# Decay masks from matrix products, or from differences of running sums: one change to a two-layer recurrent trunk

## The chip, the core and the metric

The kernel runs as one program on one core of a Trainium2 chip. A core has a matrix engine (TensorE, "PE" in the profile, with its weight loads shown apart as "PEld"), a vector engine (VectorE, "DVE"), an activation engine (ScalarE, "ACT"), a general engine (GpSimd, "POOL") and a sequencer that here only issues transfers (SyncE, "SP"). Each engine works through its own list of instructions in order and waits on semaphores for the others. The metric is the device time of one execution in microseconds (us); lower is better. Before the change it is 2958.59 us, the median of three runs (2957.11 to 2960.16).

## The reference

Two decoder layers are computed for 256 tokens of width 2048, in float32. Layer 0 mixes an HGRN2 head group with a gated-DeltaNet head group (8 heads), layer 1 is a Mamba-2 SSD mixer (64 heads in 8 groups of 8). Each layer then cross-attends into 256 memory tokens and applies a SwiGLU feed-forward block.

Both the DeltaNet and the SSD part need, for each head, a decay mask: with log-decays `g` of the tokens, token `i` sees token `j <= i` with the factor `exp(g[j+1] + ... + g[i])`, and tokens after it not at all. The reference writes that as a difference of running sums, chunk by chunk:

```python
acum = jnp.cumsum(ac, axis=-1)
lower = jnp.tril(jnp.ones((CHUNK, CHUNK), bool))
lmat = jnp.exp(jnp.where(lower, acum[..., :, None] - acum[..., None, :], -jnp.inf))
cb = jnp.einsum('zbign,zbjgn->zbgij', cc, bc)
y_diag = jnp.einsum('zbgrij,zbjgrp->zbigrp', cb[:, :, :, None] * lmat, xc)
```

The kernel covers the 256 tokens as two halves of 128 (index `a`), so it needs three 128x128 blocks per head: half 0 on half 0, half 0 on half 1, and half 1 on half 1. A block has the earlier token `j` on the partitions and the later token `i` along the row.

## The kernel before

Most of the program is a stream of weight tiles. `wtiles` (L160 and on) loads 512 KB of raw weights through SP's queue into `wr`, ACT rounds them to the reduced float32 format (`wh`, the cast recorded at L157), and DVE takes the remainder (`wl`, the subtraction recorded at L125). There are four buffers of each. `xstat` multiplies 128 tokens of activations, also split into two parts (`u`), with every tile: per tile of 1024 columns a row, twelve matmuls of 128x512 into two accumulators `acc` (three products, two token halves, two k). So a weight tile can be rounded at most four tiles ahead of the matmuls that use it. All matmuls of the helper `mm` have line L122, transposes of activations L285.

Work between the weight matmuls goes to PSUM tiles `mx` (three buffers). The order on each engine is not written out by hand. The scheduler of the framework simulates a timeline while the program is recorded and emits each engine's list in that order; instructions with no stated order can move past each other, and a changed operation can thus move others.

The decay masks are made by two functions. `decay_parts(gT, n)` runs once in each mixer (n = 8 heads in DeltaNet, 64 in SSD), after the log-decays `gT` (128 tokens x 2 halves x n) are known. It splits `gT` into `gh` and `gl`, makes one column per head `cj` (the sum of the decays after token j in half 0), and for half 1 a row of running sums per head, which goes through DRAM (`rows`). `decays(gs, h0, pool_e)` makes the masks `E` (128 x 4 heads x 3 blocks x 128) of four heads. It is called twice in DeltaNet (tile `D`) and sixteen times in SSD: twice per group of 8 heads, into `D` and then into `MD`. The middle block is a broadcast of the running sums, loaded by POOL's queue straight into `E`, plus the column as the bias of an exponential (four of 128x128, L421). The two others are matrix products: DVE multiplies the decays by a triangular matrix `le`, once for `gh` and once for `gl` (four products of 128x512 into `tmp`, L125), and PE multiplies a strictly triangular matrix `gt_r` into them (four matmuls of 128x512, `mx<-tmp,mr`), so that the sums of the stretches come out in PSUM; ACT exponentiates them into `E` (L416, L419). `gt_r` and a matrix of ones lie in the tile `mr`.

In SSD, `group(g, bct)` then multiplies `E` by the products `cb` (one 128x1536 product on DVE per four heads, written `D<-D,b` or `MD<-MD,b`), and PE multiplies it with the group's values (`mx<-D,w` and `mx<-MD,w`). DVE adds the result to the skip term (`X<-cv,cols,mx`), multiplies by the gate, and ACT and DVE split it into a new `u` for the output projection, which runs after groups 3 and 7. The tag `tmp` has two buffers, and in SSD only `decays` uses it. Each group takes 16 weight tiles, 8 for the values and 8 for the gate.

Of the kernel before, what the change touches and what calls it, by code (L numbers as in the profile page):

```python
# [9 lines left out]
F32 = mybir.dt.float32  # L10
F32R = mybir.dt.float32r
U32 = mybir.dt.uint32
I32 = mybir.dt.int32
AF = mybir.ActivationFunctionType
ALU = mybir.AluOpType
# [20 lines left out]


C_ID, C_GT, C_LE = 0, 128, 256
C_LV = 384
LEVELS = (1, 2, 4, 8, 16, 32, 64)  # L40


# [26 lines left out]
def constants():  # L69
    a = np.arange(P)[:, None]  # L70
    b = np.arange(P)[None, :]
    parts = [a == b, a > b, a <= b]
    for s in LEVELS:
        parts.append(((b // s) % 2 == 1) & (a // s == b // s - 1))
    return np.concatenate([p.astype(np.float32) for p in parts], axis=1)
# [3 lines left out]
def trunk(ctx: ExitStack, tc: tile.TileContext, A: dict, out: bass.AP):  # L79
# [20 lines left out]
    le = cst[:, C_LE:C_LE + P]  # L100
    eps = cp.tile([P, 1], F32, name="eps")
    pool.memset(eps, EPS)
    mr = cp.tile([P, 2, P], F32R, name="mr")
    gt_r, ones_r = mr[:, 0, :], mr[:, 1, :]
    gt, ones = gt_r.bitcast(F32), ones_r.bitcast(F32)

    def later(ins):

        return tc.keep_in_program_order(ins)

    def constants_in():
        later(nc.sync.dma_start(cst, A["cst"][:, 0:C_LV]))
        later(nc.sync.dma_start(cols[:, KT:], A["cols"][:, KT:]))
        dve.tensor_copy(gt_r, cst[:, C_GT:C_GT + P])
        dve.tensor_scalar(ones_r, ident, 0.0, 1.0, op0=ALU.mult, op1=ALU.add)

    def col(name, i=0, n=1):
        o = COLS[name][0] + i
# [2 lines left out]
    def mm(o, lhsT, rhs, start=True, stop=True):  # L121
        return pe.matmul(o, lhsT=lhsT, rhs=rhs, start=start, stop=stop, skip_group_check=True)  # L122

    def tt(e, o, a, b, op):
        e.tensor_tensor(o, a, b, op=op)  # L125
# [4 lines left out]
    def t4(tag, shape, dt=F32):  # L130
        return mp.tile(shape, dt, name=tag, tag=tag, bufs=BUFS.get(tag, 1))

    def psb(shape=None):
        return pm.tile(shape or [P, 512], F32, name="mx", tag="mx")
# [21 lines left out]
    def split(hi, lo, src):  # L156
        act.copy(hi, src)  # L157
        tt(dve, lo, src, hi.bitcast(F32), ALU.subtract)
# [57 lines left out]
    class SquareSum:  # L216
# [17 lines left out]
        def column(self, n):  # L234

            r = cp.tile([P, 2], F32, name="r", tag="r", bufs=2)
            ps = psb([P, 2])
            for a in range(2):
                mm(ps[:, a:a + 1], self.s[:, a * P:(a + 1) * P], ones[:, 0:1])
            rsqrt(r, ps, n)  # L240
            return r

# [157 lines left out]

    def decays(gs, h0, pool_e):

        gs, cj, gr = gs
        E = t4(pool_e, [P, 4, 3, P])
        nc.gpsimd.dma_start(E[:, :, 1, :], gr[h0:h0 + 4, :].partition_broadcast(P))
        gle = []
        for a in range(2):
            g2 = t4("tmp", [P, 2, 4, P], F32R)
            for q in range(2):
                tt(dve, g2[:, q], gs[q][:, a, h0:h0 + 4].bitcast(F32).unsqueeze(2).to_broadcast([P, 4, P]),  # L410
                   le.unsqueeze(1).to_broadcast([P, 4, P]), ALU.mult)
            gle.append(g2)
        p00, p11 = psb([P, 4, P]), psb([P, 4, P])
        mm(p00, gt_r, gle[0][:, 0], True, False)
        mm(p00, gt_r, gle[0][:, 1], False, True)
        act.activation(E[:, :, 0, :], p00, AF.Exp)  # L416
        mm(p11, gt_r, gle[1][:, 0], True, False)
        mm(p11, gt_r, gle[1][:, 1], False, True)
        act.activation(E[:, :, 2, :], p11, AF.Exp)  # L419
        for m in range(4):  # L420
            act.activation(E[:, m, 1, :], E[:, m, 1, :], AF.Exp, bias=cj[:, h0 + m:h0 + m + 1])  # L421
        return E

    def decay_parts(gT, n):


        gh, gl = t4("gh", [P, 2, n], F32R), t4("gl", [P, 2, n], F32R)
        split(gh, gl, gT)
        cj = t4("cj", [P, n])
        ps = psb([P, n])  # L430
        mm(ps, gt, gT[:, 0, :])
        dve.tensor_copy(cj, ps)
        gr, gd = t4("gr", [n, P]), dp.tile([n, P], F32, name=f"rows{n}")
        ps = psb([n, P])
        mm(ps, gT[:, 1, :], le)
        act.copy(gr, ps)
        nc.gpsimd.dma_start(gd, gr)
        return (gh, gl), cj, gd

    def head_norm(o_ps, gate, yT, eps):  # L440

# [36 lines left out]
    def hybrid(N, nxt):  # L478
# [47 lines left out]
        def gdn(g):  # L526
# [3 lines left out]
            for j, dst in ((1, 0), (0, 1)):  # L530
                c = kq[:, :, dst, :]
                conv_in(j, g, c)
                if j and not heads:
                    heads.extend(small_heads())
                elif not j:
                    E = decays(heads[0], 4 * g, "D")
                    for b in (0, 2):
                        tt(dve, E[:, :, b, :], E[:, :, b, :], le.unsqueeze(1).to_broadcast([P, 4, P]), ALU.mult)
                act.activation(c, c, AF.Silu)
                sq = t4("tmp", [P, 4, T])  # L540
                act.activation(sq, c, AF.Square)
                for a in range(2):
                    for m in range(4):
                        mm(nps[:, dst, a, m:m + 1], sq[:, m, a * P:(a + 1) * P], ones[:, 0:1])
            if g == 0:
                levels_in()

# [500 lines left out]
```

## Time and profile before

| what | value |
| --- | --- |
| median of three runs | 2958.59 us (2957.11 to 2960.16) |
| the profiled execution, time | 2957.01 us |
| the profiled execution, span | 2955.2 us |
| mean granted TensorE clock | 0.998 |
| PE busy | 2929.2 us (99% of the span) |
| PE weight loads busy | 2432.1 us (82%) |
| DVE busy | 1781.8 us (60%) |
| ACT busy | 1518.5 us (51%) |
| transfers, mean | 182 GB/s |

The span runs from the first to the last instruction; the profiled time holds another 1.8 us around it. A matmul's recorded duration is longer than its share of the engine, since matmuls overlap: in a stretch of back-to-back work, what one costs is read from the distance between starts, not from the duration in the groups. The mask work lies in two places: at about 56 to 75 us and around 257 us (DeltaNet, groups 0 and 1), and from about 1440 to 2030 us (SSD).

### The profile page before, as it was taken

Reading aid. Unit: us, or ns where it says so; the run is one execution under the profiler, and the core shown is the slowest. Engines: PE = TensorE matmul, PEld = TensorE weight load, DVE = VectorE, ACT = ScalarE, POOL = GpSimd, SP = SyncE. Lnnn points to the kernel's source line nnn. Section 1 sums busy time; section 2 is a strip of 40 time slices with the busy share of each in tenths; the row PEclk is TensorE's granted clock in tenths of the full one; section 3 lists DMA queues with packets and bytes.
Section 4 is the critical chain, followed back from the end, with each engine's and each line's share of the span. In section 5 each row is a group of like instructions: output and inputs, shape, how many; then the busy total and the mean of one; then the engine's idle time right before and its main releaser. Section 6 shows DMA issues by size and latency. Waiting matters only on the chain.

```text
span 2955.2 us, 36490 instructions
## 1 busy us (share of the span) xinstructions
PE 2929.2 (99%) x13916; PEld 2432.1 (82%) x13916; DVE 1781.8 (60%) x2320; ACT 1518.5 (51%) x1942; POOL 34.3 (1%) x57
## 2 busy tenths in 40 slices
PE   9999999999999999999999999999999999999998
PEld 7888888788888888888888788878888888888887
DVE  6676768766554445545677746777665454455455
ACT  7445446555443443444667645766554444443444
POOL 0000000000000000000000000000000000000000
PEclk9999999999999999999999999999999999999999
DMA  8555544456665566665655566555666666666664
GB/s 284 169 173 158 183 137 134 143 181 190 189 189 193 192 188 191 194 190 184 187 171 165 171 193 185 170 164 168 195 193 185 192 188 193 191 190 192 193 187 148
DMA packets 153664, 538.11 MB, mean 182 GB/s; under 512 B 16920, under 2 KB 23200, under 8 KB 153488
## 3 DMA queue, kind: packets, MB, share of 16 engines
q1 hardware_dynamic: 150096, 526.15, 57.0%
q0 software_dynamic: 2976, 9.35, 1.0%
q8 instruction: 109, 1.79, 0.2%
q14 instruction: 67, 0.55, 0.1%
q10 hardware_dynamic: 416, 0.27, 0.0%
HBM read 531.21 MB, written 4.49 MB: 181 GB/s over the span
## 4 chain that ended last, share of the span: by engine, by line
PE 97%; DVE 1%; ACT 1%; DMA 1%; issue 0%; SPq 0%; DVEq 0%; ACTq 0%; POOLq 0%
PE acc L122 89%; PE mx L122 5%; PE mx L285 1%; PE tn L285 1%; DMA wr<-in_hy_w_in 0%; DVE wl L125 0%; ACT wh L157 0%; PE mx L884 0%; DVE tmp L125 0%; DMA D<-rows 0%; ACT b L313 0%; DMA rows<-gr 0%; DVE b L128 0%; PE mx L453 0%; DVE h L125 0%
## 5 line engine op out<-in xcount | busy, mean ns | idle before, releaser
L122 PE MATMUL acc<-wh,u 128*128 128x512 f32 (+1 forms) x7904 | 2448.5, 389 | 6.9 <-ACT wh L157 6.5
L125 DVE TENSOR_TENSOR wl<-wr,wh 128x1024 fp32r<-128x1024 f32 x980 | 1197.9, 1224 | 990.3 <-ACT wh L157 986.6
L122 PEld LDWEIGHTS acc<-wh,u 128*128 128x128 f32 x7904 | 1474.4, 188 | 306.3 <-ACT wh L157 6.5
L157 ACT CAST wh<-wr 128x1024 fp32r<-128x1024 f32 x980 | 1029.1, 1052 | 1140.1 <-PE acc L122 1089.9
L122 PE MATMUL acc<-wl,u 128*128 128x512 f32 (+1 forms) x3952 | 1538.6, 389 | 0.9 <-DVE wl L125 0.8
L122 PEld LDWEIGHTS acc<-wl,u 128*128 128x128 f32 x3952 | 743.4, 188 | 150.5 <-DVE wl L125 2.0
L128 DVE SCALAR_TENSOR_TENSOR cv<-tn,cols,cv 128x255 f32<-128x255 f32 (+2 forms) x120 | 57.5, 479 | 10.9 <-ACT cv L363 8.0
L125 DVE TENSOR_TENSOR h<-h,acc 128x512 f32<-128x512 f32 (+1 forms) x92 | 57.7, 657 | 9.8 <-PE acc L122 9.5
L371 ACT ACTIVATE raw<-acc,r 128x512 f32<-128x512 f32 x66 | 43.5, 685 | 29.9 <-PE acc L122 28.2
L128 DVE SCALAR_TENSOR_TENSOR u<-mx,cols,u 128x256 fp32r<-128x256 f32 x96 | 43.1, 478 | 6.6 <-ACT u L306 5.4
L285 PE MATMUL tn<-cst,raw 128*128 128x128 f32 x272 | 45.3, 272 | 0.4 <-DVE vt L128 0.4
L306 ACT ACTIVATE u<-mx,cols 128x256 fp32r<-128x256 f32 x80 | 35.0, 469 | 20.9 <-PE mx L285 17.8
L285 PEld LDWEIGHTS tn<-cst,raw 128*128 128x128 f32 x272 | 34.4, 140 | 9.9 <-issue 0.8
L125 DVE TENSOR_TENSOR u<-mx,u 128x512 fp32r<-128x512 f32 x48 | 31.0, 684 | 13.3 <-ACT u L157 13.3
L157 ACT CAST u<-mx 128x512 fp32r<-128x512 f32 x48 | 26.0, 593 | 17.2 <-PE mx L285 10.6
L313 ACT ACTIVATE b<-h 128x512 f32<-128x512 f32 x48 | 29.9, 624 | 1.3 <-DVE h L128 1.3
L125 DVE TENSOR_TENSOR tmp<-gh,cst 128x512 fp32r<-128x512 f32 x36 | 24.6, 686 | 7.6 <-PE mx L122 7.6
L122 PEld LDWEIGHTS mx<-tmp 128*128 128x128 f32 x240 | 28.1, 192 | 0.6
L122 PE MATMUL mx<-tmp 128*128 128x64 f32 (+1 forms) x240 | 27.9, 273 | 0.0
L285 PE MATMUL mx<-cst,h 128*128 128x128 f32 x160 | 25.6, 272 | 0.0
L128 DVE SCALAR_TENSOR_TENSOR X<-cv,cols,mx 128x256 f32<-128x256 f32 x32 | 14.0, 478 | 18.5 <-PE mx L122 18.5
L122 PE MATMUL mx<-tmp,mr 128*128 128x512 f32 x72 | 24.9, 427 | 0.0
(272 smaller groups left out, 1254.5 us busy)
## 6 DMA issues: line engine op xcount, KB each, us to landing
wr<-in_ffn_w_gate SPq DMA_DIRECT2D x176, 512.0 KB, 3.7
wr<-in_ffn_w_up SPq DMA_DIRECT2D x176, 512.0 KB, 3.7
wr<-in_ffn_w_down SPq DMA_DIRECT2D x176, 512.0 KB, 3.6
wr<-in_ssd_w_in SPq DMA_DIRECT2D x162, 512.0 KB, 3.7
wr<-in_hy_w_in SPq DMA_DIRECT2D x130, 512.0 KB, 3.8
wr<-in_ssd_w_out SPq DMA_DIRECT2D x64, 512.0 KB, 3.7
wr<-in_hy_w_out SPq DMA_DIRECT2D x32, 512.0 KB, 3.7
wr<-in_xa_wq SPq DMA_DIRECT2D x16, 512.0 KB, 3.7
```

What stands on the lines that cost most here:

```text
L122: return pe.matmul(o, lhsT=lhsT, rhs=rhs, start=start, stop=stop, skip_group_check=True)
L125: e.tensor_tensor(o, a, b, op=op)
L128: dve.scalar_tensor_tensor(o, a, s, b, op0=op0, op1=op1)
L157: act.copy(hi, src)
L285: pe.transpose(ps[:, x, a * P:(a + 1) * P], src[a][:, c * P:(c + 1) * P], ident)
L306: act.activation(hi[:, c], ps[:, x], AF.Copy, scale=g)
L313: act.activation(t4("b2", [P, 512]), src[:, a], AF.Square, accum_out=self.ss[:, a, nb:nb + 1])
L371: act.activation(o[a], accs[a], func, scale=r[:, a:a + 1])
```

## The change

Both functions are rewritten. `decay_parts` now makes running sums that restart every 64 tokens: as rows for both halves (`gr`, n x 2 x 128, through DRAM as before), and as six columns per head (`gs`): for each half and each chunk of 64 later tokens, minus the running sum of token j where j lies in that chunk, the sum left after j in its own chunk where j lies in the chunk before, and for half 0 on half 1 the sum of all that lies between j and the chunk. Four constant matrices produce them on PE in plain float32: `csum`, `rest` and `half` are new constants, `gt` existed. They lie in the tile `cst`, and a new transfer on POOL's queue brings the three. `mr` and the two DVE instructions that filled it are gone; `ones` is a column set by POOL.

`decays` loads the rows of both halves into a `tmp` tile `R` (512 KB on chip in place of 256 KB), adds the columns with two DVE instructions (1024 and 512 elements a row), clamps the first and third block at zero with a third (1024 elements), and takes one exponential over 1536 elements. What lies above the diagonal is clamped and later masked as before. No matmul is left in it.

```diff
 def constants():
     a = np.arange(P)[:, None]
     b = np.arange(P)[None, :]
-    parts = [a == b, a > b, a <= b]
+    same = a // 64 == b // 64
+    parts = [a == b, a > b, a <= b, (a <= b) & same, (a > b) & same, (a < 64) & (b >= 0)]
...
-    mr = cp.tile([P, 2, P], F32R, name="mr")
-    gt_r, ones_r = mr[:, 0, :], mr[:, 1, :]
-    gt, ones = gt_r.bitcast(F32), ones_r.bitcast(F32)
+    gt, csum, rest, half = (cst[:, c:c + P] for c in (C_GT, C_SUM, C_REST, C_HALF))
+    ones = cp.tile([P, 1], F32, name="ones")
+    pool.memset(ones, 1.0)
...
     def constants_in():
-        later(nc.sync.dma_start(cst, A["cst"][:, 0:C_LV]))
+        later(nc.sync.dma_start(cst[:, 0:C_SUM], A["cst"][:, 0:C_SUM]))
+        nc.gpsimd.dma_start(cst[:, C_SUM:], A["cst"][:, C_SUM:C_LV])
         later(nc.sync.dma_start(cols[:, KT:], A["cols"][:, KT:]))
-        dve.tensor_copy(gt_r, cst[:, C_GT:C_GT + P])
-        dve.tensor_scalar(ones_r, ident, 0.0, 1.0, op0=ALU.mult, op1=ALU.add)
...
     def decays(gs, h0, pool_e):
-        gs, cj, gr = gs
-        E = t4(pool_e, [P, 4, 3, P])
-        nc.gpsimd.dma_start(E[:, :, 1, :], gr[h0:h0 + 4, :].partition_broadcast(P))
-        gle = []
-        for a in range(2):
-            g2 = t4("tmp", [P, 2, 4, P], F32R)
-            for q in range(2):
-                tt(dve, g2[:, q], gs[q][:, a, h0:h0 + 4].bitcast(F32).unsqueeze(2).to_broadcast([P, 4, P]),
-                   le.unsqueeze(1).to_broadcast([P, 4, P]), ALU.mult)
-            gle.append(g2)
-        p00, p11 = psb([P, 4, P]), psb([P, 4, P])
-        mm(p00, gt_r, gle[0][:, 0], True, False)
-        mm(p00, gt_r, gle[0][:, 1], False, True)
-        act.activation(E[:, :, 0, :], p00, AF.Exp)
-        mm(p11, gt_r, gle[1][:, 0], True, False)
-        mm(p11, gt_r, gle[1][:, 1], False, True)
-        act.activation(E[:, :, 2, :], p11, AF.Exp)
-        for m in range(4):
-            act.activation(E[:, m, 1, :], E[:, m, 1, :], AF.Exp, bias=cj[:, h0 + m:h0 + m + 1])
+        gs, gr = gs
+        R, E = t4("tmp", [P, 4, 2, P]), t4(pool_e, [P, 4, 3, P])
+        nc.gpsimd.dma_start(R, gr[h0:h0 + 4].partition_broadcast(P))
+        s = gs[:, :, h0:h0 + 4].rearrange("p c m -> p m c")
+        by64 = lambda x, c: x.rearrange("p m a (c i) -> p m (a c) i", i=64) if c == 4 else \
+            x.rearrange("p m (c i) -> p m c i", i=64)
+        tt(dve, by64(E[:, :, 0:2], 4), by64(R, 4), s[:, :, 0:4].unsqueeze(3).to_broadcast([P, 4, 4, 64]), ALU.add)
+        tt(dve, by64(E[:, :, 2], 2), by64(R[:, :, 1], 2), s[:, :, 4:6].unsqueeze(3).to_broadcast([P, 4, 2, 64]), ALU.add)
+        dve.tensor_scalar(E[:, :, ::2], E[:, :, ::2], 0.0, None, op0=ALU.min)
+        act.activation(E, E, AF.Exp)
         return E

     def decay_parts(gT, n):
-        gh, gl = t4("gh", [P, 2, n], F32R), t4("gl", [P, 2, n], F32R)
-        split(gh, gl, gT)
-        cj = t4("cj", [P, n])
-        ps = psb([P, n])
-        mm(ps, gt, gT[:, 0, :])
-        dve.tensor_copy(cj, ps)
-        gr, gd = t4("gr", [n, P]), dp.tile([n, P], F32, name=f"rows{n}")
-        ps = psb([n, P])
-        mm(ps, gT[:, 1, :], le)
+        gr, gd = t4("b2", [n, 2, P]), dp.tile([n, 2, P], F32, name=f"rows{n}")
+        ps = psb([n, 2, P])
+        for a in range(2):
+            mm(ps[:, a], gT[:, a], csum)
         act.copy(gr, ps)
         nc.gpsimd.dma_start(gd, gr)
-        return (gh, gl), cj, gd
+        gs = t4("gs", [P, 6, n])
+        ps = psb([P, 6, n])
+        mm(ps[:, 0:2], csum, gT)
+        mm(ps[:, 2:4], rest, gT)
+        mm(ps[:, 4], gt, gT[:, 0])
+        mm(ps[:, 5], gt, gT[:, 0], True, False)
+        mm(ps[:, 5], half, gT[:, 1], False, True)
+        act.activation(gs[:, 0::4], ps[:, 0:2], AF.Copy, scale=-1.0)
+        act.activation(gs[64:P, 1::4], ps[64:P, 0:2], AF.Copy, scale=-1.0)
+        act.copy(gs[0:64, 1::4], ps[0:64, 2:4])
+        act.copy(gs[:, 2:4], ps[:, 4:6])
+        return gs, gd
```

The change also moves instructions. On PE, this is what stood around the mask products of one SSD group (`mx<-D,w`, four heads), with the matmuls that make the masks of the next four heads among them:

```order
L122 MATMUL acc<-wh,u 128x512
L122 MATMUL mx<-D,w 64x256
L122 MATMUL mx<-tmp,mr 128x512
L122 MATMUL mx<-D,w 64x128
L122 MATMUL mx<-D,w 64x256
...
L122 MATMUL mx<-D,w 64x128
L122 MATMUL mx<-tmp,mr 128x512 x3
L122 MATMUL acc<-wh,u 128x512
```

The products of the other four heads (`mx<-MD,w`) followed some three weight tiles later. Now both sets stand in one run, with nothing else between them (the lines of the helper have moved down by one):

```order
L123 MATMUL acc<-wh,u 128x512
L123 MATMUL mx<-D,w 64x256
L123 MATMUL mx<-MD,w 64x256
L123 MATMUL mx<-D,w 64x128
...
L123 MATMUL mx<-MD,w 64x256
L123 MATMUL mx<-MD,w 64x128
L123 MATMUL mx<-gate,vt 128x256
L123 MATMUL acc<-wh,u 128x512
```

Each group thus has one such run in place of two. The two other matmuls `mx<-tmp,mr` of each half mask, which stood alone or in pairs within the weight stream, are gone as well.

On DVE, at the same place (from the first reading of those products, `X<-cv,cols,mx`, to the next subtraction for a weight tile, `wl`), this stood before:

```order
L125 TENSOR_TENSOR wl<-wr,wh 128x1024 x2
L128 SCALAR_TENSOR_TENSOR X<-cv,cols,mx 128x256 x2
L125 TENSOR_TENSOR tmp<-gh,cst 128x512
L125 TENSOR_TENSOR tmp<-gl,cst 128x512
L125 TENSOR_TENSOR tmp<-gh,cst 128x512
L125 TENSOR_TENSOR tmp<-gl,cst 128x512
L125 TENSOR_TENSOR X<-X,tn 128x512
L125 TENSOR_TENSOR MD<-MD,b_11451 128x1536
L125 TENSOR_TENSOR wl<-wr,wh 128x1024
```

Now all the masks of the next group are made there:

```order
L126 TENSOR_TENSOR wl<-wr,wh 128x1024 x2
L129 SCALAR_TENSOR_TENSOR X<-cv,cols,mx 128x256 x2
L126 TENSOR_TENSOR D<-tmp,gs 128x4x256
L126 TENSOR_TENSOR D<-tmp,gs 128x4x128
L126 TENSOR_TENSOR X<-X,tn 128x512
L129 SCALAR_TENSOR_TENSOR X<-cv,cols,mx 128x256 x2
L126 TENSOR_TENSOR MD<-tmp,gs 128x4x256
L126 TENSOR_TENSOR MD<-tmp,gs 128x4x128
L413 TENSOR_SCALAR D<-D 128x4x2x128
L126 TENSOR_TENSOR wl<-wr,wh 128x1024
```

The multiplication by `cb` has moved some tiles further on. On PE, the first matmul that reads the `wl` of the last row stands 41 weight matmuls behind the run of mask products.

More of the change, by code (lines that the diff above doesn't have):

```diff
@@ L38 @@
 C_ID, C_GT, C_LE = 0, 128, 256
-C_LV = 384
+C_SUM, C_REST, C_HALF = 384, 512, 640
+C_LV = 768
 LEVELS = (1, 2, 4, 8, 16, 32, 64)
@@ L238, in column @@
             for a in range(2):
-                mm(ps[:, a:a + 1], self.s[:, a * P:(a + 1) * P], ones[:, 0:1])
+                mm(ps[:, a:a + 1], self.s[:, a * P:(a + 1) * P], ones)
             rsqrt(r, ps, n)
@@ L543, in gdn @@
                     for m in range(4):
-                        mm(nps[:, dst, a, m:m + 1], sq[:, m, a * P:(a + 1) * P], ones[:, 0:1])
+                        mm(nps[:, dst, a, m:m + 1], sq[:, m, a * P:(a + 1) * P], ones)
             if g == 0:
```

## Prediction

> **What bounds the kernel now.** I read the page's shares and its chain of waits first, then the waits of PE alone, then stretches of PE's timeline.
>
> ```profile
> span 2955.2 us, 36490 instructions
> PE 2929.2 (99%) x13916; PEld 2432.1 (82%) x13916; DVE 1781.8 (60%) x2320; ACT 1518.5 (51%) x1942; POOL 34.3 (1%) x57
> PE 97%; DVE 1%; ACT 1%; DMA 1%; issue 0%; SPq 0%; DVEq 0%; ACTq 0%; POOLq 0%
> ...
> PE acc L122 <- ACT wh L157: 6.5, 1, 6.5
> PE mx L453 <- DVE b L128: 4.6, 2, 4.4
> ```
>
> PE is 97% of the chain. Its two longest waits are the start of the kernel (6.5 us, one wait) and 4.6 us at a head norm; the masks are not among them. So a PE instruction that goes away is worth its full spacing, while an instruction saved on DVE (60%) or ACT (51%) is worth nothing, unless PE waits for it. Two questions remain: how much PE time leaves, and whether the order that the scheduler now writes makes PE wait.
>
> **PE: what leaves.** The group is
>
> ```profile
> L122 PE MATMUL mx<-tmp,mr 128*128 128x512 f32 x72 | 24.9, 427 | 0.0
> ```
>
> 72 matmuls, four for each of 18 mask calls. The 427 ns overlap their neighbours; the price is the distance of starts. Within the weight stream (PE's timeline: start, duration, work):
>
> ```profile
> 2010.37 0.39 PE L122 MATMUL acc<-wh,u 128*128 128x512 f32 x1
> 2010.59 0.62 PE L122 MATMUL mx<-tmp,mr 128*128 128x512 f32 x2
> 2011.05 0.39 PE L122 MATMUL acc<-wh,u 128*128 128x512 f32 x1
> 2011.28 0.40 PE L122 MATMUL acc<-wl,u 128*128 128x512 f32 x1
> ```
>
> Two take 0.46 us, 0.23 each, as much as a weight matmul (2011.05 to 2011.28). At that price 72 are 16.6 us. But in SSD half of them stand among the mask products, which run in plain float32:
>
> ```profile
> 1975.35 0.65 PE L122 MATMUL mx<-D,w 128*64 128x256 f32 x2
> 1975.93 0.49 PE L122 MATMUL mx<-tmp,mr 128*128 128x512 f32 x1
> 1976.35 1.52 PE L122 MATMUL mx<-D,w 128*64 128x128 f32 x14
> 1977.80 0.97 PE L122 MATMUL mx<-tmp,mr 128*128 128x512 f32 x3
> 1978.61 0.40 PE L122 MATMUL acc<-wh,u 128*128 128x512 f32 x1
> ...
> 2037.27 1.57 PE L122 MATMUL mx<-MD,w 128*64 128x256 f32 x16
> 2038.77 0.96 PE L122 MATMUL acc<-wh,u 128*128 128x512 f32 x3
> ```
>
> Sixteen products with nothing between them take 1.50 us (2037.27 to 2038.77). The same sixteen with four mask matmuls among them take 3.26 us (1975.35 to 1978.61), so those four cost 1.76 us, 0.44 each: the alternation of the two number formats costs time too. In the new order both sets stand in one run, which I price at 2 x 1.50. A group then saves 1.76 us plus its four other matmuls at 0.23 (0.92), 2.68 us; eight groups save 21.4 us, the two DeltaNet calls 8 x 0.23 = 1.8. **Together 23.2 us leave.** The bounds: 16.6 us if alternation is not saved, 23.2 if it is; I take the second, since the new order has no such matmul left.
>
> **PE: what comes.** The column sums grow, as PE records, from 4 to 14 per mixer (a float32 `mm` shows as two).
>
> ```profile
> 56.26 0.28 PE L122 MATMUL mx<-gT,mr 128*128 128x8 f32 x2
> 56.47 0.39 PE L122 MATMUL mx<-cst,gT 128*8 128x128 f32 x2
> 56.78 0.73 PE L122 MATMUL acc<-wh,u 128*128 128x512 f32 x2
> ...
> 1438.98 0.33 PE L122 MATMUL mx<-gT,mr 128*128 128x64 f32 x2
> 1439.24 0.43 PE L122 MATMUL mx<-cst,gT 128*64 128x128 f32 x2
> 1439.60 0.50 PE L122 MATMUL acc<-wh,u 128*128 128x512 f32 x1
> ...
> 178.60 1.05 PE L122 MATMUL mx<-X,b 128*128 128x128 f32 x8
> 179.49 1.06 PE L122 MATMUL mx<-b,X 128*128 128x128 f32 x8
> ```
>
> Four took 0.52 us with 8 heads and 0.62 with 64, so 0.13 to 0.155 each; in a longer run, eight took 0.89 (178.60 to 179.49), 0.11 each. Ten more per mixer are 1.1 to 1.55 us; I take **+2.8 us** for both (2.2 to 3.1).
>
> The Trainium skill (FP8 and Floating Point Precision, TensorE Precision Notes) gives true float32 four passes through the array. The eight products per 128x128 step at 178.60 fit it (0.89 us for four matmuls of 128 columns, 0.22 each, what a reduced-format matmul of 512 columns takes). The mask products don't: sixteen records, 4 x 256 plus 4 x 128 columns, would be an estimated 2.8 us by it, and the trace has 1.50. By columns and passes alone the new sums would add an estimated 1.2 us in place of 2.8, and the total would be 1.6 us lower.
>
> **DVE and ACT: the masks.** Row for row, in starts of DVE's timeline:
>
> ```profile
> 1977.91 0.87 DVE L128 SCALAR_TENSOR_TENSOR X<-cv,cols,mx 128x256 f32<-128x256 f32 x2 [1.50 <-PE mx L122]
> 1978.70 0.68 DVE L125 TENSOR_TENSOR tmp<-gh,cst 128x512 fp32r<-128x512 f32 x1
> 1979.30 0.69 DVE L125 TENSOR_TENSOR tmp<-gl,cst 128x512 fp32r<-128x512 f32 x1
> ...
> 1983.38 1.22 DVE L125 TENSOR_TENSOR wl<-wr,wh 128x1024 fp32r<-128x1024 f32 x1
> 1984.51 0.87 DVE L128 SCALAR_TENSOR_TENSOR u<-X,cols,u 128x256 fp32r<-128x256 f32 x2
> 1985.30 0.42 DVE L125 TENSOR_TENSOR b<-b 128x256 f32<-128x256 f32 x1
> ...
> L657 DVE TENSOR_SCALAR kq<-kq,lbs 128x256 f32<-128x256 f32 x8 | 2.4, 346 | 0.5 <-ACT kq L655 0.4
> L995 DVE TENSOR_SCALAR h<-h,r 128x512 f32<-128x512 f32 x5 | 2.1, 481 | 0.6 <-ACT r L988 0.6
> L701 DVE COPY_PREDICATED D<-big,mx 128x512 f32<-128x512 uint32 x14 | 12.4, 888 | 5.0 <-PE mx L122 4.9
> ```
>
> Before, a mask of four heads took four products at 0.60 us: 2.4. Now it takes an add of 1024 elements (1.13, as `wl`), one of 512 (0.60; both operands of `tmp<-gh,cst` were broadcasts too, without a surcharge) and a clamp of 1024. The trace has no clamp of that size; on the line from 346 (256 elements) to 481 ns (512) it is 0.75, as a two-tensor instruction 1.22. I take 0.75, being nearest in kind: 2.5 us. DVE neither gains nor loses, and ACT takes one exponential for six. I cost both at nothing; PE's weight stream is the cover, and the place where it could run out is the one that the order shows. There, between the first mask products and the next `wl`, DVE now has two pairs `X<-cv,cols,mx` (0.79 a pair), four adds (3.46 for both halves), one `X<-X,tn` (0.60), a clamp (0.75) and the `wl` itself (1.2): 7.6 us from the end of the `D` products. The run's last eight products, at 0.09 each, are still under way in the first 0.75 us of it, so `wl` is ready 6.9 us after the run. PE meanwhile has 41 weight matmuls at 0.23, 9.4 us. DVE has 2.5 us to spare, so nothing is late. With every add at the worst ratio that the strided row above has (888 against 684 for a plain one, 1.3), four adds take 1.0 us more, and still nothing. I take **+0.5 us** for small waits that the new order may hold (0 to 8, the latter if each group loses 1 us).
>
> **Transfers.** `R` is twice as large as the broadcast before, but goes into `tmp`, which in SSD only the adds hold, and not into a mask tile that PE reads to the last:
>
> ```profile
> L405 POOL DMA_DIRECT2D D<-rows x10: 747/747/776, 60.2 to 1978.2; - x10
> ...
> D<-rows POOLq DMA_DIRECT2D x10, 256.0 KB, 4.1
> ```
>
> It can be issued as soon as the previous group's add is done, 16 tiles of twelve matmuls (2.8 us each) ahead of its own; 0.75 us to issue and 4.1 to land, even doubled, are hidden. The three new constants (128 x 384 floats, 192 KB) are not: POOL issues them in the first microseconds, beside the tile that PE starts on.
>
> ```profile
> 6.54 1.22 PE L122 MATMUL acc<-wh,u 128*128 128x512 f32 x2 [6.54 <-ACT wh L157]
> ...
> GB/s 284 169 173 158 183 137 134 143 181 190 189 189 193 192 188 191 194 190 184 187 171 165 171 193 185 170 164 168 195 193 185 192 188 193 191 190 192 193 187 148
> ```
>
> At the first slice's 284 GB/s they are 0.7 us. PE's start may slip by 0 to 0.7; I take **+0.4 us**.
>
> **The sum.** -23.2 + 2.8 + 0.5 + 0.4 = -19.5 us. Against the profiled execution (2957.0 us around a span of 2955.2) that is 2937.5; the median of the runs, 2958.6, lies 1.6 above it, so I forecast **2939 us** as a median, 0.66% faster.
>
> **The rivals.**
>
> *Alternation stays (2946 us).* If the formats' change is paid by the run of mask products as a whole and not by the matmuls among them, only 16.6 leave: -16.6 + 3.7 = -12.9. For it: a run of products still stands between reduced-format matmuls on both sides. Against: 1.50 and 3.26 us above.
>
> *New waits eat half of it (2948 to 2956 us).* The masks of a group are now made in one piece on DVE; if its lead over PE is smaller than the order suggests, each group loses 1 to 2 us behind a late `wl`, 8 to 16 in all. For it: only four tiles of lead exist. Against: the 2.5 us to spare, and that before, 5.5 us without a `wl` at the same place (1977.91 to 1983.38) cost PE nothing.
>
> *Slower (2997 us): the broadcast comes late.* DVE takes its work in order, so an add that waits for `R` holds the next `wl`, and PE behind it. If POOL, disturbed by DVE, got each transfer out only when DVE had stopped at the add itself, the add would wait 0.75 + 4.1 us. That is 9.7 us for the two halves of a group, less the 2.5 to spare: 7.2 us in each of eight groups, 58 in all, and 58 - 19.5 = +38. It decides once `R` is late by 4.9 us per group (2.5 + 19.5 / 8). For it: DVE is the busiest helper in these groups. Against: before, POOL issued in 747 to 776 ns all the time, beside a DVE that is 60% busy. The Trainium skill (SBUF — State Buffer, SBUF: two separate sides) says that a DVE instruction which uses both ports locks POOL out of writing descriptors, and the clamp may be one; the row of 776 ns at most gives no sign of it.
>
> *The change doesn't do what it says*: the new order of PE holds no `mx<-tmp,mr`, so there is little room for that; it would leave 2959 us.
>
> **Chances.** Forecast (2933 to 2943) 0.60; alternation stays (2943 to 2948) 0.20; new waits 0.13, split at the bound; slower 0.05; anything else that cancels the gain 0.02. Of this kernel a change of 0.2%, 5.9 us, can be told from none; faster than 2952.7 holds the first two and half of the third: 0.86; within 0.2% 0.09; slower 0.05. The lower end of the range is all of 23.2 us with the cheaper column sums and nothing else, 2936, less the spread of the median, 2933; the upper end takes in the waits to 2950.
>
> **What would show it.** PE's records without `mx<-tmp,mr`; a run of 32 mask records in some 3.0 us (against it: 3.8); PE's list of waits with no entry on `wl` or on `D` beyond 1 us each; `R` landed long before its add (against it: DVE idle for the transfer, tens of us); the clamp near 0.75 us; PE's first matmul at 6.5 to 7.2 us. A DVE or ACT that is less busy with the same end would not count for me: I said it is worth nothing. I am wrong if PE's busy time falls by 20 us and its idle time grows by as much.

## The result, and the profile after

The changed kernel takes **2938.55 us** (median of six runs, 2937.37 to 2939.55) beside 2959.89 us for the kernel before in the same session (2957.11 to 2961.31). The ratio is 0.9929 with a 95% interval of 0.9919 to 0.9939: 0.7% faster, 21.3 us. The prediction was 2939 us.

The page of the changed kernel, its totals and the chain by engine:

```profile
span 2937.7 us, 36230 instructions
PE 2911.8 (99%) x13864; PEld 2425.5 (83%) x13864; DVE 1776.5 (60%) x2296; ACT 1461.5 (50%) x1825; POOL 31.1 (1%) x59
...
PE 98%; DVE 1%; ACT 1%; issue 0%; DMA 0%; SPq 0%; DVEq 0%; ACTq 0%
```

PE has 52 records fewer (72 mask matmuls gone, 20 records of column sums more) and is busy 17.4 us less; the span is 17.5 us shorter. That is less than the 21.3 us of the medians because each page shows a single execution: the one of before (2957.01 us) lies 2.9 us below its median, the one of after (2939.53 us) 1.0 above. ACT lost 57 us and DVE 5 us, which are off the path. Most of ACT's part is not exponentials but `ACT_TABLE_LOAD`, 1283 ns each, of which 81 became 48 (42 us). The largest group of them before and after, at the first exponential of a mask:

```profile
L416 ACT ACT_TABLE_LOAD x17 | 21.8, 1283 | 0.3
...
L414 ACT ACT_TABLE_LOAD x10 | 12.8, 1283 | 0.2
```

Who PE waited for, in the changed kernel (total, times, longest):

```profile
PE acc L123 <- ACT wh L158: 6.7, 1, 6.7
PE mx L453 <- DVE b L129: 4.3, 1, 4.3
PE mx L123 <- DVE D L790: 1.3, 1, 1.3
PE acc L123 <- DVE wl L126: 1.1, 2, 0.9
```

No new wait on a mask or on a late `wl` came up (`wl` has 1.1 us in two waits, and had 1.3 us in two before; L790 is another part of the program). To see where the time went I cut both traces at the first and the last start of one matmul that both have, in the DeltaNet part and behind the SSD part. The view of that tile, in the kernel before (durations, then first and last start):

```profile
L122 PE MATMUL mx<-D,XT x16: 379/379/454, 649.3 to 2188.9; 128*128 128x256 f32 x16
```

The same row of the changed kernel:

```profile
L123 PE MATMUL mx<-D,XT x16: 379/379/454, 650.9 to 2170.6; 128*128 128x256 f32 x16
```

This middle stage holds all SSD masks. It went from 1539.6 to 1519.7 us, **-19.9**. The rest of the trace hardly moved: the front +1.6 in this execution (649.2 in another one of the same kernel), the end +0.8 (766.3 to 767.1). The view by stretches, of the kernel before (length, then busy PE, PEld, DVE, ACT and POOL):

```profile
649.30:2188.90 1539.60, 1538.66 (x7208) 1268.37 (x7209) 927.73 (x1121) 823.16 (x1066) 12.54 (x17) 1.00 0.59 183
```

Of the changed kernel:

```profile
650.90:2170.60 1519.70, 1519.11 (x7153) 1259.93 (x7154) 923.34 (x1103) 768.12 (x957) 9.10 (x17) 1.00 0.57 188
```

PE is idle 0.9 us in it before and 0.6 after: of this stage's gain all but 0.3 us is PE work that is gone. The run of mask products of one group, and the column sums of DeltaNet, in PE's timeline of the changed kernel (start, duration, work):

```profile
56.42 0.39 PE L123 MATMUL acc<-wl,u 128*128 128x512 f32 x1
56.74 0.60 PE L123 MATMUL mx<-cst,gT 128*8 128x128 f32 x4
57.27 1.28 PE L123 MATMUL mx<-gT,cst 128*128 128x16 f32 x10
58.41 0.48 PE L123 MATMUL acc<-wh,u 128*128 128x512 f32 x1
...
2018.18 0.39 PE L123 MATMUL acc<-wh,u 128*128 128x512 f32 x1
2018.50 0.65 PE L123 MATMUL mx<-D,w 128*64 128x256 f32 x2
2018.98 0.38 PE L123 MATMUL mx<-MD,w 128*64 128x256 f32 x1
2018.99 0.43 PE L123 MATMUL mx<-D,w 128*64 128x256 f32 x1
2019.20 0.38 PE L123 MATMUL mx<-MD,w 128*64 128x256 f32 x1
2019.25 1.25 PE L123 MATMUL mx<-D,w 128*64 128x256 f32 x13
2020.28 1.52 PE L123 MATMUL mx<-MD,w 128*64 128x128 f32 x14
2021.73 0.50 PE L123 MATMUL acc<-wh,u 128*128 128x512 f32 x1
```

32 product records take 3.23 us (2018.50 to 2021.73) where two separate sets, one of them with four mask matmuls in it, took 3.26 + 1.50. The fourteen records of column sums take 1.67 us (56.74 to 58.41) where four took 0.52. The masks on DVE, in the groups of the changed kernel (busy and mean, then idle time ahead):

```profile
L126 DVE TENSOR_TENSOR D<-tmp,gs 128x1024 f32<-128x1024 f32 x10 | 12.2, 1220 | 2.1 <-DMA tmp<-rows 1.7 <-PE mx L123 0.4
L126 DVE TENSOR_TENSOR D<-tmp,gs 128x512 f32<-128x512 f32 x10 | 6.8, 684 | 0.0
L413 DVE TENSOR_SCALAR D<-D 128x1024 f32<-128x1024 f32 x10 | 6.8, 685 | 0.0
```

The issue of `R` (a `tmp`), in the view of that tile:

```profile
L407 POOL DMA_DIRECT2D tmp<-rows x18: 531/531/578, 61.9 to 1922.2; - x18
```

Its landing, in the view of the transfers (KB, then us from issue to landing):

```profile
tmp<-rows POOLq DMA_DIRECT2D x18, 512.0 KB, 4.1
```

An add of 1024 elements takes what a `wl` does, the clamp 685 ns. DVE waited 1.7 us in all for `R`, which still lands in 4.1 us at twice the size.

### The profile page after: what moved, and what is told of

It reads as the page before. It is cut to its first block, busy times and chain, and to the rows that moved or that the text cites. A ratio compares the mean times of both kernels' runs of the same rounds, so it can differ in the third digit from the quotient of the medians.

```text
span 2937.7 us, 36230 instructions
## 1 busy us (share of the span) xinstructions
PE 2911.8 (99%) x13864; PEld 2425.5 (83%) x13864; DVE 1776.5 (60%) x2296; ACT 1461.5 (50%) x1825; POOL 31.1 (1%) x59
## 4 chain that ended last, share of the span: by engine, by line
PE 98%; DVE 1%; ACT 1%; issue 0%; DMA 0%; SPq 0%; DVEq 0%; ACTq 0%
PE acc L123 91%; PE mx L123 5%; PE mx L286 1%; PE tn L286 1%; DVE wl L126 0%; PE mx L884 0%; ACT wh L158 0%; DVE tmp L126 0%; DMA wr<-in_hy_w_in 0%; PE mx L453 0%; DVE h L126 0%; DVE b L129 0%; PE mx L563 0%; DVE h L995 0%; ACT XT L372 0%
## 5 line engine op out<-in xcount | busy, mean ns | idle before, releaser
L307 ACT ACTIVATE u<-mx,cols 128x256 fp32r<-128x256 f32 x80 | 35.2, 470 | 19.6 <-PE mx L286 16.2
L129 DVE SCALAR_TENSOR_TENSOR kq<-tn,cols,kq 128x255 f32<-128x255 f32 (+2 forms) x48 | 22.9, 477 | 2.7 <-ACT kq L364 1.9
L286 PEld LDWEIGHTS mx<-cst,h 128*128 128x128 f32 x160 | 20.1, 140 | 5.0
L613 ACT COPY b<-mx 128x512 f32<-128x512 f32 x12 | 7.0, 586 | 29.7 <-PE mx L123 29.7
```

Of the source, the lines that this page charges most:

```text
L129: dve.scalar_tensor_tensor(o, a, s, b, op0=op0, op1=op1)
L286: pe.transpose(ps[:, x, a * P:(a + 1) * P], src[a][:, c * P:(c + 1) * P], ident)
L307: act.activation(hi[:, c], ps[:, x], AF.Copy, scale=g)
L613: act.copy(R, ps)
```

## The experiments

All kernels sent together ran on the same chip with the kernel before; r1 to r12 went in four sessions behind that of the result (r1 to r4; r5 to r8; r9 to r11; r12), and across sessions the ratio and the middle stage compare better than the medians. The table gives medians, the ratio to the kernel before, and the middle stage as cut above. "64-column stretches" is a count that I made from the records of each trace between 1400 and 2200 us: how many uninterrupted stretches of matmuls with 64 columns of weights there are (the mask products `mx<-D,w` and `mx<-MD,w`, and one small stretch of column sums), and how long PE spent in them. That column was made last, after all the runs. "Stretches of float32" in the expectations is another count, of plain float32 work between reduced-format matmuls, in PE's order: 273 before, 253 after.

| run | median us | ratio to before | middle stage us | 64-column stretches, time in them |
| --- | --- | --- | --- | --- |
| before | 2959.89 | 1 | 1539.6 | 25, 28.6 us |
| after | 2938.55 | 0.9929 | 1519.7 | 9, 26.4 us |
| r1, after again | 2938.63 | 0.9931 | 1519.7 | 9, 26.4 |
| r9, after again | 2939.06 | 0.9926 | 1519.8 | 9, 26.4 |
| r2, 72 matmuls back | 2962.15 | 1.0011 | 1539.5 | 25, 28.8 |
| r8, 144 matmuls | 2980.66 | 1.0072 | 1554.1 | 25, 28.8 |
| r3, 64 reduced ones between heads | 2991.37 | 1.0109 | 1572.5 | 72, 52.4 |
| r11, 64 plain ones between heads | 2990.79 | 1.0103 | 1572.1 | 72, 52.4 |
| r12, 64 plain ones of 64 columns | 2954.33 | 0.9985 | 1535.3 | 24, 39.2 |
| r7, before, masks ahead | 2965.62 | 1.0022 | 1545.1 | 25, 28.6 |
| r10, one tile for B and C | 2937.93 | 0.9925 | 1519.0 | 9, 26.4 |
| r4, DVE more | 2945.46 | 0.9955 | 1525.4 | 9, 26.4 |
| r5, six exponentials | 2937.82 | 0.9928 | 1519.8 | 9, 26.4 |
| r6, rows into the mask | 2937.97 | 0.9930 | 1519.0 | 9, 26.4 |

### The base again

> The changed kernel unchanged, beside the runs that follow: 2938.5 us, 0.993 of the kernel before. It is the base of the others.

> The changed kernel again, as the base for the two runs sent with it. 2938 to 2939.5 us.

2938.63 and 2939.06 us. Kernels within about 1 us of each other are not told apart below. Between single executions of the changed kernel the front, up to the middle stage, differs by 1.7 us (649.2 and 650.9) and the middle stage by 0.1, so small differences are read from the middle stage.

### The 72 matmuls put back, and put back twice

The masks stay as in the changed kernel; four matmuls of 128x512 in the reduced format are added behind each mask's exponential, on constant data, their result unused (`gz` is the identity, rounded).

```diff
         act.activation(E, E, AF.Exp)
+        for q in range(2):
+            pz = psb([P, 4, P])
+            mm(pz, gz, gz.unsqueeze(1).to_broadcast([P, 4, P]), True, False)
+            mm(pz, gz, gz.unsqueeze(1).to_broadcast([P, 4, P]), False, True)
         return E
```

> The changed kernel with 72 matmuls of 128x512 in the reduced format put back (four per mask call, on constant data, their result unused), so that only PE's work returns; they land among the mask products of four heads as before. Theory (PE's time alone was removed, 0.44 us for each matmul among the mask products and 0.23 for the others): +21 to +23 us, 2960. Rival 'alternation costs nothing' (0.23 each): +16.6, 2955. Rival 'the gain came from ACT or DVE': +5 at most, under 2944.

2962.15 us, +23.5 on r1, and a middle stage as long as before. PE's timeline of this run around the products of four heads:

```profile
1534.57 0.39 PE L125 MATMUL acc<-wh,u 128*128 128x512 f32 x1
1534.89 0.65 PE L125 MATMUL mx<-D,w 128*64 128x256 f32 x2
1535.46 0.50 PE L125 MATMUL mx<-gz 128*128 128x512 f32 x1
1535.90 1.52 PE L125 MATMUL mx<-D,w 128*64 128x128 f32 x14
1537.35 0.96 PE L125 MATMUL mx<-gz 128*128 128x512 f32 x3
1538.15 0.39 PE L125 MATMUL acc<-wh,u 128*128 128x512 f32 x1
```

The scheduler put the dead matmuls where the mask matmuls had stood, one behind the first product and three behind the last: 3.26 us from 1534.89 to 1538.15, to the hundredth what the prediction's rows of the kernel before have. So the 72 matmuls alone are worth the gain, while DVE and ACT stay as little busy as in the changed kernel (ACT 1463.7 us for the 1461.5 there and 1518.5 before). With `range(4)` in the loop:

> The changed kernel with 144 matmuls put back, eight per mask call. Theory (all of it is PE time): the first 72 as in the run with 72, the second 72 outside the products at 0.23, +38 to +40 us, 2978. Rival 'there is room on PE for some of it': the second 72 cost less than 10 us.

2980.66 us: the second 72 cost 18.5 us, 0.26 each (0.23 each in the middle stage: 14.6 us for 64). They stand beside the first, and 25 stretches stay 25: an added matmul that breaks nothing costs its own time.

### A reduced-format matmul between every two heads

In the changed kernel, a dead matmul behind each head's two products, held there by an order (`behind`).

```diff
-                    mm(o, xd[:, 0, hd], E[:, m, 0:2]..., m // 2 == 0, False)
-                    mm(o[:, P:T], xd[:, 1, hd], E[:, m, 2], False, True)
+                    i0 = mm(o, xd[:, 0, hd], E[:, m, 0:2]..., m // 2 == 0, False)
+                    if last is not None:
+                        behind(i0, last)
+                    i1 = mm(o[:, P:T], xd[:, 1, hd], E[:, m, 2], False, True)
+                    last = mm(pz, gz, gz.unsqueeze(1).to_broadcast([P, 4, P]), m == 0, m == 3)
+                    behind(last, i1)
```

> The changed kernel with 64 such matmuls in SSD, one held behind each head's two mask products and ahead of the next head's. The list of PE then changes between the two number formats 69 times more often. Theory (a change of format costs): at 0.44 each +28 us, 2967. Rival 'alternation costs nothing': 64 x 0.23, +14.7, 2953.

+52.7 us, 0.82 each, nearly twice what the theory gave. Something at those places costs far more than the 0.44 of the prediction, which was a mean over one isolated matmul and three in a row. At this point I still read it as the price of changing the number format, now some 0.6 us a change and back.

### Both masks of a group ahead of the products, in the kernel before

```diff
+            Es = [decays(gs, 8 * g + 4 * half, ("D", "MD")[half]) for half in range(2)]
             for half in range(2):
-                E = decays(gs, 8 * g + 4 * half, ("D", "MD")[half])
+                E = Es[half]
```

> The kernel before with the masks of both halves of a group made ahead of the products of either, so that no mask matmul stands among the products; matmuls, casts and exponentials as before. Theory (a matmul among the products costs 0.44 in place of 0.23): 8 x 0.84 = -6.7 us, 2953. Rival 'alternation costs nothing': 2960.

+6.5 us where -6.7 was expected. The mask matmuls did leave the products, and yet the products did not get cheaper. PE's timeline of this run:

```profile
1529.86 0.65 PE L122 MATMUL mx<-D,w 128*64 128x256 f32 x2
1530.43 0.49 PE L122 MATMUL acc<-wh,u 128*128 128x512 f32 x1
1530.86 1.52 PE L122 MATMUL mx<-D,w 128*64 128x128 f32 x14
1532.31 0.50 PE L122 MATMUL acc<-wl,u 128*128 128x512 f32 x1
1532.64 0.63 PE L122 MATMUL acc<-wh,u 128*128 128x512 f32 x2
1533.20 1.57 PE L122 MATMUL mx<-MD,w 128*64 128x256 f32 x16
```

What is new among PE's waits in this run:

```profile
PE mx L884 <- ACT cv L879: 4.5, 8, 0.6
...
PE mx L122 <- DMA XT<-scratch: 2.2, 1, 2.2
```

A weight matmul now stands behind the first product, and the two sets are still apart: per group stretches of 2, 14 and 16 records, exactly as before. Nothing was saved there. The two new waits come to 6.7 us: 4.5 lie in the middle stage, which grew by 5.5, and 2.2 ahead of it, where this execution took 5.0 us more than the one of before, so they are not shown to be all of the difference. The run does not test what it was made for; by the count of stretches it is no miss.

### DVE, ACT and the broadcast

Two clamps of 1024 elements more per mask (at 30, without effect); six exponentials per mask in place of one; the rows loaded straight into `E`, without the early load into `tmp`.

```diff
+        dve.tensor_scalar(E[:, :, 0:2], E[:, :, 0:2], 30.0, None, op0=ALU.min)   # r4, twice
         act.activation(E, E, AF.Exp)
```

```diff
-        act.activation(E, E, AF.Exp)
+        act.activation(E[:, :, 0, :], E[:, :, 0, :], AF.Exp)   # r5
+        act.activation(E[:, :, 2, :], E[:, :, 2, :], AF.Exp)
+        for m in range(4):
+            act.activation(E[:, m, 1, :], E[:, m, 1, :], AF.Exp)
```

```diff
-        R, E = t4("tmp", [P, 4, 2, P]), t4(pool_e, [P, 4, 3, P])   # r6
-        nc.gpsimd.dma_start(R, gr[h0:h0 + 4].partition_broadcast(P))
+        E = t4(pool_e, [P, 4, 3, P])
+        nc.gpsimd.dma_start(E[:, :, 0:2, :], gr[h0:h0 + 4].partition_broadcast(P))
...
```

In r6 the two adds then read `E` in place of `R`, the one for the third block first.

> The changed kernel with two more clamps of 1024 elements (against 30, which alters nothing) in each mask call: some 1.3 us more of DVE per call, 2.6 us per SSD group, 23 us in all, as large as what I said DVE has to spare behind a group's mask products. Theory (DVE is covered): 0 to +3 us, 2938 to 2942. Rival 'DVE's list sets PE's pace there': up to +23, 2961.

> The changed kernel with six exponentials per mask call, as before the change, in place of one. Theory (ACT is covered): no change, 2937 to 2940. Rival 'part of the gain came from ACT': some 0.9 us more per call, up to +16 us.

> The changed kernel with the row sums loaded straight into the mask tile, so that the transfer can't start until PE has read the mask before. Theory (the broadcast is hidden in any case, since a mask is needed some ten weight tiles after it is made): 0 to +3 us, 2938 to 2942. Rival 'the prefetch into tmp carried the result': each add waits 0.5 + 4.1 us behind the products, up to 7 us for each of eight groups, +37 to +56.

r5 and r6 are within 0.8 us of r1 (ratios 0.9928 and 0.9930 for 0.9931): the exponentials and the early load are worth nothing here. r5 tests the exponentials alone. It adds 6.8 us to ACT's busy time (1468.3 for 1461.5) and no table loads; that the other 50 us are worth nothing is shown by r2, which has the time of before without them. In r6 DVE does wait for the rows:

```profile
DVE D L126 <- DMA D<-rows: 15.6, 10, 2.8
```

With 0.6 us more for `MD` these are 16.2 us, and PE's list of waits has no entry that the base lacks. So waits of DVE of this size are covered. The 4.6 us per add that the rival of the late broadcast needs (+37 us and more) did not come up, since no wait was over 2.8 us.

r4 costs 6.8 us, more than the theory's 3 and far less than the rival's 23. In its middle stage PE is idle 3.6 us (0.6 in the base); the view by stretches of this run:

```profile
651.10:2176.50 1525.40, 1521.79 (x7153) 1261.07 (x7154) 940.42 (x1135) 770.21 (x959) 9.06 (x17) 1.00 0.56 187
```

Two of PE's waits are new in it:

```profile
PE tn L286 <- DVE cv L129: 1.6, 1, 1.6
PE acc L123 <- ACT raw L372: 1.4, 2, 1.1
```

None of them is at the products, where the prediction had its 2.5 us to spare. The scheduler plans all lists anew when an operation is added, so what a busier DVE costs cannot be read off one place. The two waits are the 3.0 us of new idle time, of the 5.7 us by which the stage grew; the other 2.7 are busy time of PE with the same 7153 records, and where they arise I did not trace.

### The format theory tried on its own

If a change between reduced and plain float32 costs about 0.6 us, three things follow: joining two plain products in the weight stream gains, a plain float32 matmul between the heads is cheap, and a reduced one is dear (r3). In the changed kernel the second product of B and C (`mx<-gate,vt`, 128x128) stands alone, some 17 weight matmuls behind the first. Writing both to one PSUM tile brings them together.

```diff
-            p0 = psb([P, 2, P])
-            mm(p0, Bt[:, 0:P], Ct)
-            p1 = psb([P, P])
-            mm(p1, Bt[:, P:T], Ct[:, P:T])
+            pc = psb([P, 3, P])
+            mm(pc[:, 0:2], Bt[:, 0:P], Ct)
+            mm(pc[:, 2], Bt[:, P:T], Ct[:, P:T])
```

> The changed kernel, with the two products of B and C of a group (mx<-gate,vt, 128x256 and 128x128) written to one PSUM tile, so that they stand together on PE. In the changed kernel the second stands alone, some 17 weight matmuls behind the run of mask products; PE's order now holds 245 stretches of plain float32 in place of 253, with the same matmuls. Theory (a stretch of plain float32 among reduced-format matmuls costs about 0.4 to 0.6 us beside its own work): 8 stretches less give -3 to -5 us, about 2934 to 2936. Rival (the alternation costs only where reduced matmuls stand among the mask products, not in the weight stream): no change, 2938 to 2939.5.

2937.93 us beside 2939.06, ratios 0.9925 and 0.9926: no change, the rival's figure (the middle stage is 0.8 us shorter, 0.1 for each of the eight joined, where 0.4 to 0.6 was expected). And r3 with `gz` in plain float32, 128x128 in place of 128x512:

```diff
-    gz = cp.tile([P, P], F32R, name="gz")
+    gz = cp.tile([P, P], F32, name="gz")
...
-                    last = mm(pz, gz, gz.unsqueeze(1).to_broadcast([P, 4, P]), m == 0, m == 3)
+                    last = mm(pz, gz, gz, m == 0, m == 3)
```

> The run r3 once more (64 dead matmuls, one behind each head's two mask products), but each dead matmul is one of 128x128 in plain float32 (two records) and no longer one of 128x512 in the reduced format. Alone such a matmul costs about 0.22 us, as much as the other. Theory (the change of the number format is what costs): 64 x 0.22 = 14, and PE's order has seven more stretches of float32 at 0.5, 3.5: in all +16 to +19 us, and about 0.6 us from one head to the next in the run of products. Rival (any foreign matmul between two mask products, with other weights and another shape, costs as much): 64 x 0.82 as in r3, +50 to +55 us, 1.2 us from head to head.

+51.7 us: **the format theory falls**. No format changes there any more, and the price is that of r3. PE's timeline of this run:

```profile
1531.71 0.86 PE L125 MATMUL mx<-D,w 128*64 128x256 f32 x4
1532.50 0.49 PE L125 MATMUL mx<-gz 128*128 128x128 f32 x2
1532.92 0.86 PE L125 MATMUL mx<-D,w 128*64 128x256 f32 x4
1533.71 0.49 PE L125 MATMUL mx<-gz 128*128 128x128 f32 x2
```

One head's four records take 0.79 us (1531.71 to 1532.50) where sixteen in a row take 1.50, 0.375 a head; the dead matmul takes 0.42 in place of 0.22. Together 0.79 + 0.42 - 0.375 = 0.84 per matmul, 53 us for 64. So the time of the products themselves had doubled. In the code, head `m` writes the output partitions `64 * (m % 2)` and up: two neighbouring heads, I concluded, fill different halves of the array's columns. And in the changed kernel's timeline above two records of 64 columns start at 2018.98 and 2018.99, though one of 256 columns alone takes 0.22. The new theory: products of two heads in different halves run side by side, and a matmul of 128 columns among them ends that. It can be told from "any foreign matmul" by making the dead one 64 columns wide:

```diff
-                    last = mm(pz, gz, gz, m == 0, m == 3)
+                    last = mm(pz[64 * (m % 2):64 * (m % 2) + 64], gz[:, 0:64], gz, m < 2, m >= 2)
```

> The run r11 once more (64 dead matmuls in plain float32, one behind each head's two mask products, +51.7 us there), but each dead matmul has 64 columns of weights, as the mask products have, and writes the same half of the output partitions as the head it stands behind. New theory (a head's products have 64 columns of weights and fill half of the array's columns; the products of two neighbouring heads, in different halves, run side by side, and a matmul of 128 columns among them ends that): the dead matmul joins one of the two streams, two records of 0.11 us in each, so 0.11 to 0.15 us per matmul, 64 x 0.11 to 0.15 = +7 to +10 us, and 2946 to 2950 us. Rival (any matmul with other operands between two heads' products costs as much as in r3 and r11): +50 us, about 2990 us.

The middle stage is 1535.3 us, +15.5 on r9 and 36.8 less than r11, whose dead matmuls differ only in their columns and in the half of the output that they write: 0.58 us less per matmul. The timeline:

```profile
1530.94 0.27 PE L125 MATMUL mx<-gz 128*64 128x128 f32 x1
1530.95 0.38 PE L125 MATMUL mx<-D,w 128*64 128x256 f32 x1
1531.05 0.27 PE L125 MATMUL mx<-gz 128*64 128x128 f32 x1
1531.16 0.44 PE L125 MATMUL mx<-D,w 128*64 128x128 f32 x3
1531.38 0.27 PE L125 MATMUL mx<-gz 128*64 128x128 f32 x1
```

The dead record and the other head's product start 10 ns apart, and from one dead matmul to the next it is 0.44 us (1530.94 to 1531.38) against 1.21 in r11 (1532.50 to 1533.71). The rival (+50) falls. The forecast of +7 to +10 was too low, because it left out that the order cuts the groups' runs in three, one of them in two (24 stretches in place of 9). The stretches themselves took 12.8 us more (39.2 less 26.4), of which 64 x 0.11 are 7.0; fifteen more entries and exits at some 0.2, as worked out below, are 3.0. That makes 15.8 for the 15.5 measured, but the other 5.8 us within the stretches I did not trace.

That two heads' products in the same half would lose the pairing without any other matmul between them was not run; it rests on r11, where a head alone takes 0.79 us, and on the starts.

## Why the prediction was right, and where it was wrong

**The bound** held: PE at 99%, its work worth its spacing, ACT's 57 us worth nothing (r2 has the time of before without them).

**What leaves, -23.2 us:** the size is confirmed. The middle stage lost 19.9 us in spite of 1.2 more of column sums, so 21.1 left it where 21.4 was forecast, and r2 puts 23.5 back. The split was right too: 0.23 for a matmul in the weight stream (r8), more among the mask products.

**The cause of the 0.44 was wrong.** The prediction's step "the alternation of the two number formats costs time too" fails: r11 costs the same without any such alternation, r10 saves stretches of float32 and gains nothing, and r12 takes most of the cost away by the number of columns. In its place: the products of two heads run side by side in the two halves of the array, and an interruption by a full-width matmul costs, besides that matmul, an exit and an entry and, where it parts two heads, the pair. The rows of before that the prediction shows hold it already. Their 3.26 us are 0.58 for the first two records, 0.42 for the single mask matmul, 1.45 for fourteen records and 0.81 for the three mask matmuls. So the four mask matmuls took 1.23 where 0.92 is their price in the weight stream, and the products 2.03 where they take 1.50 in one piece: most of the loss lies in the first product, alone, which held PE from 1975.35 to 1975.93, 0.58 us for two records that in the run take 0.25 (a row of 16 in 1.50, of which those of 256 columns take two thirds). The price of a stretch comes from r2: its middle stage is 19.8 us longer than r1's, 64 matmuls at 0.23 are 14.7, and 5.1 are left for sixteen more stretches, 0.32 each. (Of the 23.5 us between the medians another 1.8 are the eight matmuls of DeltaNet at 0.23; the last 1.9 lie outside the middle stage and are not explained.)

That also answers the Trainium skill's rule that the prediction weighed and set aside (FP8 and Floating Point Precision, TensorE Precision Notes: four passes for true float32). By it sixteen product records would be an estimated 2.8 us, and the trace had 1.50. The Trainium skill (TensorEngine Tiling (Array Packing), Performance Considerations) also states that weights of 64 columns allow two-fold column tiling: half of 2.8 is an estimated 1.4, and the runs agree (1.50 in pairs, 0.79 for one head alone with its entry and exit, which is 3.2 for four).

Put together, for the middle stage: 64 matmuls at 0.23 are 14.7, the products' own stretches 8 x (0.58 + 1.45 + 1.50 - 3.23) = 2.4, sixteen entries and exits at some 0.2 (the 0.42 less 0.23 above) 3.2, less 1.2 for the column sums: 19.1 of the 19.9 measured. Of the last 0.8, PE's idle time explains 0.3; the rest is open.

**What comes.** The column sums cost 1.15 us with 8 heads (1.67 less 0.52), or 1.2 with the slower step into and out of them. With 64 heads they cost 1.2 counted in that way (from the weight matmul ahead to the second one behind, 2.36 us in the changed kernel from 1440.41 to 1442.77, less 1.19 before, from 1438.75 to 1439.94). That is 2.4 together for the 2.8 taken. PE's first matmul starts at 6.65 us for 6.54, +0.1 for the 0.4 taken. New waits: PE's list sums to 14.0 us (the two entries not shown above are 0.3 each) for 14.9 before, so -0.9 for the +0.5 taken; no mask and no product waits. These three terms err by 0.4, 0.3 and 1.4 us on the same side: -23.2 + 2.4 + 0.1 - 0.9 = -21.6, where -19.5 was forecast and -21.3 came. That the forecast of 2939 lies 0.4 us from the median is therefore in part luck: the kernel before ran at 2959.89 in the session of the result and not at the 2958.59 from which the forecast was counted.

**Two bounds of the range** do not come out of its working. The lower end, 2936, was counted from the profiled execution (2957.0 - 23.2 + 2.2), where the forecast was counted from the median; from that it is 2937.6. And the upper end "takes in the waits to 2950", while the range ends at 2943. Neither matters for the result.

**DVE** was costed at nothing, by a clamp of 0.75 us (0.685 measured), adds at 1.13 and 0.60 (their records are 1.22 and 0.68, as before for the same shapes), and a spare 2.5 us per group. Nothing was late. But r4 shows that "spare at one place" is no measure: 25 us more of clamps on DVE (36 at 0.69), 1.4 per mask, cost 6.8 us at other places.

**The rivals.** "Alternation stays" (2946) had the right instinct in its for-line, that the run of products as a whole pays at its ends, but one run per group in place of three is what the new order brought, and the time fell accordingly. "New waits" did not occur. "The broadcast comes late" falls by `R`'s 4.1 us to land, POOL's 531 to 578 ns per issue, 1.7 us of waiting in all, and by r6, where 16.2 us of waiting cost nothing.

**Its test by the run of 32 records** (3.0 for the forecast, 3.8 against) gave 3.23. The part over 3.0 is unpaired work at the start of the run: the first two records, a first head without its partner, take 0.48 (2018.50 to 2018.98).

## What to carry to other kernels

Before pricing a matmul by its own length, look at what stands on both sides: products with 64 columns of weights that write different halves of the output partitions run in pairs, and a full-width matmul among them costs the pair besides its own time, here 0.82 us in place of 0.22. So count the uninterrupted stretches of such products in PE's order before and after a change, and keep them in one piece, whatever the number format of what would come between. When a mean price (0.44) comes from unlike places (one alone, three in a row), split it before building a cause on it.

## What was not expected of the hardware

- Two mask products in different column halves start some 10 ns apart and each keeps its own pace (0.22 us for a record of 256 columns): sixteen records in 1.50 us, a single head's four in 0.79.
- A plain float32 matmul of 128x128 and a reduced-format one of 128x512, put at the same 64 places, cost the same, +51.7 and +52.7 us. By r10 a lone plain float32 product in the stream of reduced-format matmuls costs at most 0.1 us more than one beside others (0.8 us in the middle stage for eight).
- A full-width matmul in a run of 64-column products took 0.42 us in place of 0.23, and each further stretch of such products cost 0.32 us.
- 33 table loads of ACT fewer, 42 us of its busy time, changed nothing in the time of the kernel, as r2 shows.
- Twice the bytes of a broadcast to 128 partitions (512 KB for 256) landed in the same 4.1 us.
